# RWKV scan of a hybrid layer on one core: every product of a chunk as 64x64 tiles on the array's diagonal

## The chip, the cores and the metric

One core of one Trainium2 chip runs the whole layer in one launch. The time is device microseconds of that core. PE is the engine of the matrix products, DVE and ACT work element by element, POOL does the rest, SP issues transfers.

## The reference, cut to what matters

One layer normalises its input, projects it once, runs three kinds of heads side by side (gated DeltaNet, RWKV-7, Mamba-2) and projects their outputs back. All is float32. The change lies in the RWKV heads (8 of width 64) and, for a small part, in the DeltaNet heads (6 of width 128).

```
def rwkv7_recurrence(r, w, k, v, a, b):          # state S is 64x64 for each head
    def step(state, inp):
        sa = einsum("bhvk,bhk->bhv", state, a_t)
        state = state * w_t + sa[..., None] * b_t + v_t[..., None] * k_t
        return state, einsum("bhvk,bhk->bhv", state, r_t)
...
def gated_delta_rule(q, k, v, g, beta):          # chunks of 64; 1040 frames with the meta tokens
    a_mat = where(strict, einsum("bhnid,bhnjd->bhnij", kb, k) * dmask, 0.0)
    sol = triangular_solve(a_mat + eye(CHUNK), rhs, left_side=True, lower=True, unit_diagonal=True)
```

## The kernel before, in words

A planner (`schedule`) walks through twelve units (six of DeltaNet, a0 to a5; four of RWKV, b0 to b3, of two heads each; two of Mamba, c0 and c1) and lays their steps out in one order. The projection's products (tile `pj`, at one pass in float32r) are the filling: a unit runs until a `yield`, the planner notes how long its result will take on ACT or DVE, and puts projection products until then. The costs are counted by `Meter`; for a float32 product it counts the larger of the moving and the stationary columns over 600. A priority then decides which instruction goes ahead where several could. PE works in that order.

A unit of RWKV (`unit_b`) has two heads, which lie on the two halves of the 128 rows of its tiles: rows 0 to 63 and rows 64 to 127. It has 17 chunks of 64 frames.

- `bn`: norms of the keys, one small product for each chunk.
- `bgr`: the chunk's matrices of inner products. For each head one product of 64 rows by 128 columns, with 128 moving columns (bk against ar, where the two halves of 128 are a and r, or b and k). DVE masks them into `bgm`.
- `bbT`, `bvT`: transposes, which ACT copies out to `bbt` and `buv`.
- `solve32` inverts 32x32 blocks on DVE. The merges `bm1` and `bm2` (products of 32x32) put the inverse of 64x64 together, chunk by chunk and head after head.
- The scan runs over the chunks. Into PSUM tile `bsi` go the product of `ar` with the state (128x128, with the state of both heads as a block diagonal) and for each head a product of 64x64; ACT copies it to `b_x`; `bu` is for each head a product of 64x64; DVE scales it into `buv`; `bd` is one product of 128x128, of which only the two diagonal blocks are used; ACT and DVE make the next state `b_s` of it (one DVE instruction for each head); and a product of 128 rows by 64 columns for each head adds to the outputs, which ACT copies to `by`.

A float32 product is two records in the trace, each with its own load of the stationary matrix; a transpose or a float32r product is one. In DeltaNet (`unit_a`) the merges are `am1` to `am3` (32x32) and `am4`, `am5` (64x64). Each lane of units has two PSUM buffers (`ps`).

Of the kernel before, what the change touches and what calls it, by code (L numbers as in the profile page):

```python
# [26 lines left out]
EPS = 1e-6  # L27
# [13 lines left out]
PIPE = 0.5  # L41
# [60 lines left out]
class Trunk:  # L102
# [266 lines left out]
    def unit_a(self, h):  # L369
        nc, sm = self.nc, self.sm  # L370
        v, act, pe, pool, sync = self.engines
        ident = self.ident
# [16 lines left out]
        lo3 = lo[:, NM:].rearrange("p (c t) -> p c t", c=8)  # L389
# [24 lines left out]
        bd = sm.tile([128, 9], F32, tag="a_bd", name="a_bd", bufs=3)  # L414
# [80 lines left out]
        yield  # L495
        v1 = dvf[:, 512:768], dvf[:, 0:256]
        fs = [(slice(64 * i, 64 * i + 32), slice(64 * i + 32, 64 * i + 64)) for i in range(2)]
        for i, (f, s) in enumerate(fs):
            p = self.ps(f"am1{h}_{i}")
            for c in range(8):  # L500
                pe.matmul(p[s, 32 * c: 32 * c + 32], lo3[f, c, s], dd[f, c, 0:32], start=True, stop=True)
            act.copy(v1[i][s], p[s, 0:256])
            yield 0.6
        for i, (f, s) in enumerate(fs):
            p = self.ps(f"am2{h}_{i}")
            for c in range(8):
                pe.matmul(p[f, 32 * c: 32 * c + 32], v1[i][s, 32 * c: 32 * c + 32], lo3[s, c, s], start=True, stop=True)
            act.copy(lo3[f, :, s], p[f, 0:256].rearrange("p (c t) -> p c t", c=8))
            if i == 0:
                yield 0.6  # L510
                p = self.ps(f"am3{h}")
                for c in range(8):
                    pe.matmul(p[s, 32 * c: 32 * c + 32], lo3[s, c, s], v1[0][s, 32 * c: 32 * c + 32], start=True, stop=True)
                act.copy(dd[s, :, 0:32], p[s, 0:256].rearrange("p (c t) -> p c t", c=8))
                yield 0.3
        yield

        f, s = slice(0, 64), slice(64, 128)
# [122 lines left out]
    def unit_b(self, p):  # L641
# [43 lines left out]

        ar, bk = ([self.one([128, 9 - i, 128], f"b{x}{p}_{i}") for i in range(2)] for x in ("ar", "bk"))

        ib = sm.tile([64, 17, 2], F32, tag="b_ib", name="b_ib")
        for i, (s, e) in enumerate(split):
            act.activation(bk[i][:, :, 0:64], k[:, s:e], AF.Square, scale=self.kk[:, p: p + 1])  # L690
        yield
        ps = self.ps(f"bn{p}")
        for c in range(17):
            pe.matmul(ps[0:64, 2 * c: 2 * c + 2], at_c(bk, c)[:, 0:64], self.blk[:, 0:65:64], start=True, stop=True)
        v.tensor_scalar(ib, ps[0:64, 0:34].rearrange("p (c h) -> p c h", h=2), EPS, None, ADD)
# [13 lines left out]
        yield 11  # L709
        self.calm = False  # L710

        gms = [[self.one([128, 9 - i, 128], f"bgm{p}_{h}{i}") for i in range(2)] for h in range(2)]
        gm = lambda h, c: at_c(gms[h], c)
        banks = ((1, 5), (5, 9), (9, 13), (13, 17), (0, 1))
        hs = (slice(0, 64), slice(64, 128))
        for s, e in banks:
            for h in range(2):
                ps = self.ps(f"bgr{p}_{h}{s}")
                for c in range(s, e):
                    pe.matmul(ps[:, 128 * (c - s): 128 * (c - s) + 128], at_c(bk, c)[hs[h]], at_c(ar, c)[hs[h]], start=True, stop=True)  # L720
                v.tensor_tensor(gms[h][s // 9][:, s % 9: s % 9 + e - s, :], ps[:, : 128 * (e - s)].rearrange("p (c t) -> p c t", c=e - s),
                                bc(self.maskb, 1, e - s), MUL)
                yield PIPE
        for h in range(2):
            for i, (s, e) in enumerate(split):
                ab = gms[h][i][0:64, :, 0:64]
                nc.vector.tensor_tensor(ab, ab, bc(ib[:, s:e, h], 2, 64), MUL)
# [9 lines left out]
        blocks = [(34 * h + 17 * b + s, e - s, gms[h][i][32 * b: 32 * b + 32, :, 32 * b: 32 * b + 32])  # L737
                  for h in range(2) for b in range(2) for i, (s, e) in enumerate(split)]
        for o, n, t in blocks:
            nc.sync.dma_start(d1[o: o + n].rearrange("c i j -> i c j"), t)  # L740
# [17 lines left out]
        for c in range(0, 17, 4):  # L758
            cc = range(max(c - 3, 0), c + 1)
            ps = self.ps(f"bvT{p}_{c}")  # L760
            for j in range(0, len(cc), 2):
                pe.transpose(ps[: 64 * min(2, len(cc)), 64 * j: 64 * j + 128], v_[:, 64 * cc[j]: 64 * (cc[j] + min(2, len(cc)))], ident)
            for j, x in enumerate(cc):
                h = slice(64 * (j % 2), 64 * (j % 2) + 64)
                act.copy(at_c(uv, x)[64:128], ps[h, 64 * (j - j % 2): 64 * (j - j % 2) + 128])
            yield PIPE

        for w in range(2):
# [4 lines left out]
            yield PIPE  # L773
        yield

        dv = self.one([128, 34, 32], f"bdd{p}")
        f, s = slice(0, 32), slice(32, 64)
        for h in range(2):
            for i, (c0, c1) in enumerate(split):
                nc.vector.transpose(dv[f, 17 * h + c0: 17 * h + c1, :], gms[h][i][f, :, f])  # L780
        self.lag += 4
        yield
        for i0, n in ((0, 9), (9, 8), (17, 9), (26, 8)):
            p1 = self.ps(f"bm1{p}_{i0}")
            for i in range(i0, i0 + n):
                pe.matmul(p1[s, 32 * (i - i0): 32 * (i - i0) + 32], gm(i // 17, i % 17)[f, s], dv[f, i, :], start=True, stop=True)
            act.copy(dv[s, i0: i0 + n, :], p1[s, : 32 * n].rearrange("p (c t) -> p c t", c=n))
            yield
            p2 = self.ps(f"bm2{p}_{i0}")
            for i in range(i0, i0 + n):  # L790
                pe.matmul(p2[f, 32 * (i - i0): 32 * (i - i0) + 32], dv[s, i, :], gm(i // 17, i % 17)[s, s], start=True, stop=True)
            act.copy(gms[i0 // 17][n % 9 // 8][f, :, s], p2[f, : 32 * n].rearrange("p (c t) -> p c t", c=n))
            yield 0.1
        yield 12


        yt = self.one([128, 8, 128], f"by{p}")
        st = None
        for c in range(17):
            pq = self.ps(f"bsi{p}_{c}")  # L800
            if c:
                pe.matmul(pq[:, 0:128], at_c(ar, c), st, start=True, stop=False, skip_group_check=True)
            for h in range(2):
                pe.matmul(pq[0:64, hs[h]], gm(h, c)[64:128, 0:64], at_c(uv, c)[64:128, hs[h]],
                          start=(c == 0), stop=True, skip_group_check=True)
# [4 lines left out]
            for h in range(2):  # L810
                pe.matmul(pu[0:64, hs[h]], gm(h, c)[0:64, 0:64], x[0:64, hs[h]], start=True, stop=True)
            v.tensor_tensor(at_c(uv, c)[0:64].rearrange("p (h d) -> p h d", h=2), pu[0:64, 0:128].rearrange("p (h d) -> p h d", h=2),
                            bc(ib[:, c, :], 2, 64), MUL)
            yield
            if c < 16:
                pd = self.ps(f"bd{p}_{c}")
                pe.matmul(pd[:, 0:128], at_c(bt, c), at_c(uv, c), start=True, stop=True)
                sn = self.tmp("b_s")
                if c:
                    nc.scalar.activation(sn, st, AF.Copy, scale=wc[:, c + 1: c + 2])  # L820
                    for h in range(2):
                        v.scalar_tensor_tensor(sn[hs[h], hs[h]], pd[hs[h], hs[h]], wc[hs[h], c + 1: c + 2], sn[hs[h], hs[h]], MUL, ADD)
                else:
                    nc.gpsimd.memset(sn, 0.0)
                    for h in range(2):
                        v.tensor_scalar(sn[hs[h], hs[h]], pd[hs[h], hs[h]], wc[hs[h], c + 1: c + 2], None, MUL)
            if c:
                for h in range(2):
                    pe.matmul(pq[64:128, hs[h]], gm(h, c)[:, 64:128], at_c(uv, c)[:, hs[h]],
                              start=False, stop=True, skip_group_check=True)  # L830
                nc.scalar.copy(yt[hs[(c - 1) % 2], (c - 1) // 2, :], pq[64:128, 0:128])  # L831
                self.lag = max(0.2, self.lag - 0.21)
            if c < 16:
                st = sn
            if c == GATE:
                yield 8
                g = self.one([128, 17, 64], f"bg{p}")
                gated = self.later(36 + p, self.shifted(36 + p, 12 + p, g, gate=True), DUES[4])
                g = flat(g)
            else:  # L840
                yield
# [536 lines left out]
```

## Time and profile before

| what | before |
|---|---|
| median of 3 runs | 1480.29 us (1477.94 to 1482.15) |
| the profiled execution | 1481.04 us |
| its span, first to last instruction | 1479.3 us |
| PE busy | 1420.0 us, 96% |
| DVE, ACT, POOL busy | 65%, 48%, 12% |
| mean granted clock of PE | 0.965 |

The span is what the profile shows; 1.7 us lie around it. A product counts as busy until its result is out, and the next one starts before that, so that a busy PE may still hold pauses: start to start says more than busy time. The granted clock is 1 at 2.4 GHz and 0.5 at 1.2 GHz.

### The profile page before, as it was taken

The page shows a single profiled execution, that of the slowest core. Times are in us where ns is not written, and L with a number is a line of the kernel's source. Part 1 is how long each engine was busy: PE and PEld are TensorE (multiplying, and loading weights), DVE is VectorE, ACT ScalarE, POOL GpSimd, SP SyncE. Part 2 cuts the span into 40 slices and gives each one's busy share as a digit, 9 for nine tenths or more (in the row PEclk, how much of TensorE's full clock was granted, in tenths as well). Part 3 has the DMA queues.
Part 4 walks back from the last instruction along what each step waited for, and adds up shares of the span by engine and source line. Part 5 has one row for each costly group of instructions (what it writes and reads, how often), then busy time and mean ns, then how long its engine had stood idle before and what let it go on. Part 6 is the DMA issues. An engine that isn't in the chain of part 4 may idle for free.

```text
span 1479.3 us, 25499 instructions
## 1 busy us (share of the span) xinstructions
PE 1420.0 (96%) x9369; PEld 1228.4 (83%) x9369; DVE 961.0 (65%) x2682; ACT 704.1 (48%) x1924; POOL 172.8 (12%) x227
## 2 busy tenths in 40 slices
PE   4999999999999999899899999999999999889897
PEld 4999888888888888878778899889998978678686
DVE  7549486376658557879745788556588866642573
ACT  6465272245434462454655644544566354632530
POOL 2111000000000110111101111001222000200100
PEclk9999799799999999999979999999999999899999
DMA  7344323133222332434422243333544322643851
GB/s 228 87 116 86 82 62 73 30 61 90 58 45 58 87 80 66 114 62 93 92 76 55 51 101 76 61 72 88 142 90 94 74 39 50 203 142 98 255 195 54
DMA packets 120447, 136.25 MB, mean 92 GB/s; under 512 B 39867, under 2 KB 72379, under 8 KB 120323
## 3 DMA queue, kind: packets, MB, share of 16 engines
q1 hardware_dynamic: 102755, 102.64, 23.8%
q0 software_dynamic: 17568, 31.99, 12.9%
q8 instruction: 74, 1.21, 0.4%
q14 instruction: 50, 0.41, 0.1%
HBM read 116.99 MB, written 17.60 MB: 91 GB/s over the span
## 4 chain that ended last, share of the span: by engine, by line
PE 78%; DVE 8%; DMA 6%; ACT 5%; issue 2%; POOL 0%; SPq 0%; DVEq 0%; ACTq 0%; POOLq 0%
PE pj L97 41%; PE po L97 9%; PE bsi L97 5%; PE am L97 2%; PE bgr L97 2%; PE bu L97 2%; DMA omrw<-d_mix 1%; PE bm L97 1%; PE aops L97 1%; PE bd L97 1%; PE cdg L97 1%; PE ads L97 1%; DMA x<-in_x_dram 1%; DVE s_tmp L97 1%; PE agq L97 1%
## 5 line engine op out<-in xcount | busy, mean ns | idle before, releaser
L97 PE MATMUL pj<-hh,w 128*128 128x350 f32 (+7 forms) x2736 | 756.8, 349 | 1.8 <-DMA w<-in_wt_dram 1.6
L97 PEld LDWEIGHTS pj<-hh,w 128*128 128x128 f32 x2736 | 486.7, 192 | 24.5 <-DMA w<-in_wt_dram 2.0
L97 PE MATMUL pj<-hl,w 128*128 128x350 f32 (+7 forms) x1368 | 477.4, 349 | 0.0
L97 PEld LDWEIGHTS pj<-hl,w 128*128 128x128 f32 x1368 | 262.0, 191 | 11.8 <-issue 0.5
L153 POOL DMA_DIRECT2D w<-in_wt_dram x122 | 106.8, 876 | 853.9 <-ACT w L151 697.0
L151 ACT ACTIVATE w<-wr 128x512 fp32r<-128x512 f32 x122 | 76.8, 629 | 87.5 <-PE pj L97 86.4
L97 PE MATMUL po<-ow,omw 128*128 128x512 f32 x408 | 95.4, 395 | 4.5 <-ACT omw L1067 3.7
L97 PEld LDWEIGHTS po<-ow,omw 128*128 128x128 f32 x408 | 77.4, 191 | 22.5 <-ACT omw L1067 4.1
L97 PE MATMUL po<-ow,ome 128*128 128x512 f32 x360 | 88.9, 400 | 2.1 <-ACT ome L1067 1.9
L97 PEld LDWEIGHTS po<-ow,ome 128*128 128x128 f32 x360 | 67.2, 190 | 16.1 <-ACT ome L1067 2.5
L152 ACT CAST w<-wr 128x512 fp32r<-128x512 f32 x122 | 74.3, 609 | 0.1
L97 DVE TENSOR_TENSOR buv<-bu,b_ib 64x128 f32<-64x128 f32 x68 | 19.1, 282 | 69.5 <-PE bu L97 69.1
L97 PE MATMUL bsi<-buv,bgm 64*64 64x64 f32 (+1 forms) x528 | 62.5, 239 | 0.0
L97 DVE TENSOR_TENSOR alb<-alb,s_tmp 33x30 f32<-33x30 f32 (+9 forms) x180 | 57.0, 317 | 3.0 <-POOL alb L97 1.6
L97 DVE TENSOR_TENSOR s_tmp<-alb 33x30 f32<-33x30 f32 (+9 forms) x180 | 56.9, 316 | 1.2
L97 PEld LDWEIGHTS bsi<-buv,bgm 64*64 64x64 f32 (+1 forms) x528 | 42.7, 140 | 17.7 <-issue 2.7
L831 ACT COPY by<-bsi 64x128 f32<-64x128 f32 x64 | 16.8, 263 | 77.1 <-PE bsi L97 76.5
L97 DVE SCALAR_TENSOR_TENSOR b_s<-bd,b_wc,b_s 64x64 f32<-64x64 f32 x120 | 33.9, 283 | 29.8 <-PE bd L97 27.4
L1068 DVE TENSOR_TENSOR ome<-omre,ome 128x512 fp32r<-128x512 f32 (+2 forms) x40 | 21.7, 581 | 39.4 <-ACT ome L1067 39.4
L97 ACT COPY b_x<-bsi 64x128 f32<-64x128 f32 x68 | 17.6, 259 | 60.4 <-PE bsi L97 59.9
L184 DVE SCALAR_TENSOR_TENSOR cbc<-pj,pack,cbc 128x346 f32<-128x346 f32 (+4 forms) x72 | 40.0, 569 | 8.5 <-ACT cbc L181 7.7
L97 DVE TENSOR_TENSOR blb<-blb,s_tmp 68x30 f32<-68x30 f32 (+14 forms) x120 | 38.3, 320 | 1.5
(325 smaller groups left out, 2450.6 us busy)
## 6 DMA issues: line engine op xcount, KB each, us to landing
wr<-in_wt_dram SPq DMA_DIRECT2D x122, 256.0 KB, 3.4
w<-in_wt_dram POOLq DMA_DIRECT2D x122, 256.0 KB, 4.8
or<-in_w_out_dram SPq DMA_DIRECT2D x32, 256.0 KB, 3.3
omrw<-d_mix SPq DMA_DIRECT2D x32, 256.0 KB, 4.6
clt<-d_cs SPq DMA_DIRECT2D x24, 256.0 KB, 4.7
omre<-d_mix SPq DMA_DIRECT2D x24, 256.0 KB, 4.1
btw<-d_tw SPq DMA_DIRECT2D x8, 544.0 KB
x<-in_x_dram SPq DMA_DIRECT2D x8, 512.0 KB, 7.6
```

The source lines that it names most:

```text
L97: return op(out, *args, **kw)
L151: nc.scalar.activation(w[:, 1], raw, AF.Copy, scale=-1.0)
L152: nc.scalar.copy(w[:, 0], raw)
L153: nc.gpsimd.dma_start(w[:, 1], src, accum_op=ADD)
L184: nc.vector.scalar_tensor_tensor(acc[:, a + z: b], p[:, o + z - s: o + b - a - s], cw[:, 3 - s: 4 - s], acc[:, a + z: b], MUL, ADD)
L831: nc.scalar.copy(yt[hs[(c - 1) % 2], (c - 1) // 2, :], pq[64:128, 0:128])
L1068: nc.vector.tensor_tensor(t[:, 1], raw, t[:, 0].bitcast(F32), SUB)
```

## The change

All products of an RWKV chunk become products of 64x64, one for each head: head 0 reads rows 0 to 63 and writes partitions 0 to 63, head 1 reads rows 64 to 127 and writes partitions 64 to 127, and the two stand one after the other in the program. Both write the same PSUM bank, on their own partitions. The index of `gms` is now the half of the columns (a or r) and no longer the head; a tile holds both heads on its two halves. The state is kept as 128 rows by 64 columns. ACT copies the transposes out in pieces of 64 rows, and the outputs in two pieces. The merges of both heads stand in turn, and so do those of DeltaNet's two 64-row halves, which go to two PSUM buffers.

```diff
@@ unit_a, merges
+        pair = [self.ps(f"am1{h}_{i}") for i in range(2)]
+        for c in range(8):
+            for i, (f, s) in enumerate(fs):
+                pe.matmul(pair[i][s, 32 * c: 32 * c + 32], lo3[f, c, s], dd[f, c, 0:32], start=True, stop=True)
         for i, (f, s) in enumerate(fs):
-            p = self.ps(f"am1{h}_{i}")
-            for c in range(8):
-                pe.matmul(p[s, 32 * c: 32 * c + 32], lo3[f, c, s], dd[f, c, 0:32], start=True, stop=True)
-            act.copy(v1[i][s], p[s, 0:256])
-            yield 0.6
+            act.copy(v1[i][s], pair[i][s, 0:256])
+        yield 0.6
...
@@ unit_b, bgr
-            for h in range(2):
-                ps = self.ps(f"bgr{p}_{h}{s}")
-                for c in range(s, e):
-                    pe.matmul(ps[:, 128 * (c - s): 128 * (c - s) + 128], at_c(bk, c)[hs[h]], at_c(ar, c)[hs[h]], start=True, stop=True)
+            pair = [self.ps(f"bgr{p}_{x}{s}") for x in range(2)]
+            for c in range(s, e):
+                for x in range(2):
+                    for h in range(2):
+                        pe.matmul(pair[x][hs[h], 128 * (c - s): 128 * (c - s) + 128], at_c(bk, c)[hs[h], hs[x]], at_c(ar, c)[hs[h]],
+                                  start=True, stop=True)
...
@@ unit_b, transposes out
-            act.copy(bt[s // 9][:, s % 9: s % 9 + e - s, :], ps[:, : 128 * (e - s)].rearrange("p (c t) -> p c t", c=e - s))
+            for x in range(2):
+                for h in range(2):
+                    act.copy(bt[s // 9][hs[h], s % 9: s % 9 + e - s, hs[x]],
+                             ps[hs[x], : 128 * (e - s)].rearrange("p (c t) -> p c t", c=e - s)[:, :, hs[h]])
...
@@ unit_b, scan
+            def both(out, cols, lhs, part, rhs, start, stop):
+                for h in range(2):
+                    pe.matmul(out[hs[h], cols], lhs[hs[h], part], rhs[hs[h]], start=start, stop=stop, skip_group_check=True)
+
             pq = self.ps(f"bsi{p}_{c}")
+            both(pq, hs[0], gk, to_a, v1_, True, c == 0)
             if c:
-                pe.matmul(pq[:, 0:128], at_c(ar, c), st, start=True, stop=False, skip_group_check=True)
...
+                both(pq, hs[0], a_r, to_a, st, False, True)
+                both(pq, hs[1], gk, to_r, v1_, True, False)
+                both(pq, hs[1], a_r, to_r, st, False, False)
             x = self.tmp("b_x")
-            act.copy(x[0:64], pq[0:64, 0:128])
+            act.copy(x[:, 0:64], pq[:, 0:64])
...
+            both(pu, hs[0], gb, to_a, x[:, 0:64], True, True)
+            if c < 16:
+                pd = pu[:, 64:128]
+                both(pu, hs[1], b_k, hs[1], v1_, True, False)
+            v.tensor_scalar(u_, pu[:, 0:64], ib[:, c: c + 1], None, MUL)
...
-                pe.matmul(pd[:, 0:128], at_c(bt, c), at_c(uv, c), start=True, stop=True)
+                both(pu, hs[1], b_k, hs[0], u_, False, True)
...
-                    for h in range(2):
-                        v.scalar_tensor_tensor(sn[hs[h], hs[h]], pd[hs[h], hs[h]], wc[hs[h], c + 1: c + 2], sn[hs[h], hs[h]], MUL, ADD)
+                    v.scalar_tensor_tensor(sn[:, 0:64], pd, w_, sn[:, 64:128], MUL, ADD)
...
+                both(pq, hs[1], gb, to_r, u_, False, True)
                 for h in range(2):
-                    pe.matmul(pq[64:128, hs[h]], gm(h, c)[:, 64:128], at_c(uv, c)[:, hs[h]],
-                              start=False, stop=True, skip_group_check=True)
-                nc.scalar.copy(yt[hs[(c - 1) % 2], (c - 1) // 2, :], pq[64:128, 0:128])
+                    nc.scalar.copy(yt[hs[(c - 1) % 2], (c - 1) // 2, hs[h]], pq[hs[h], 64:128])
```

What stands on PE around chunk 10 of unit b0's scan before (`bsi0_10` is unit 0, chunk 10; a row names what is written, then moving and stationary operand, then the output's partitions and columns):

```order
L97 MATMUL bsi0_10_3061<-b_s_3048,bar0_1_1213 128x128
L97 MATMUL bsi0_10_3061<-buv0_1_2268,bgm0_01_1468 64x64
L97 MATMUL bsi0_10_3061<-buv0_1_2268,bgm0_11_1470 64x64
L97 MATMUL pj33_1_3186<-hh_79,w33_1_2950 128x386 x2
L97 MATMUL pj33_1_3186<-hl_80,w33_1_2950 128x386
L97 MATMUL bu0_10_3078<-b_x_3065,bgm0_01_1468 64x64
L97 MATMUL bu0_10_3078<-b_x_3065,bgm0_11_1470 64x64
L97 MATMUL pj33_1_3186<-hh_79,w33_1_2950 128x386
L97 MATMUL pj33_2_3256<-hh_79,w33_0_2944 128x322
L97 MATMUL pj33_2_3256<-hl_80,w33_0_2944 128x322
L97 MATMUL pj33_2_3256<-hh_79,w33_0_2944 128x322
L97 MATMUL bd0_10_3087<-buv0_1_2268,bbt0_1_1603 128x128
```

The chunk goes on with the two products into the outputs, so that it has 8 products in three shapes, with three or four of the projection between its three places.

And now, around chunk 9 and the start of chunk 10:

```order
L97 MATMUL bu0_9_3280<-b_x_3268,bgm0_01_1484 64x64 x2
L97 MATMUL bu0_9_3280<-buv0_1_2450,bbt0_1_1630 64x64 x2
L97 MATMUL pj33_1_3214<-hh_79,w33_1_3126 128x386
L97 MATMUL pj33_1_3214<-hl_80,w33_1_3126 128x386
L97 MATMUL pj33_1_3214<-hh_79,w33_1_3126 128x386
L97 MATMUL bu0_9_3280<-buv0_1_2450,bbt0_1_1630 64x64 x2
L97 MATMUL bsi0_9_3259<-buv0_1_2450,bgm0_01_1484 64x64 x2
```

Each `x2` of 64x64 is now a pair, head 0 and head 1. A chunk's 8 products became 16, in eight pairs of one shape; there are three projection products between two places here.

What stands on PE for the second bank of `bgr` of unit b0 before (`bgr0_05` is head 0, `bgr0_15` head 1, of four chunks each):

```order
L97 MATMUL pj25_2_1805<-hh_79,w25_0_1412 128x322 x2
L97 MATMUL pj25_2_1805<-hl_80,w25_0_1412 128x322
L97 MATMUL bgr0_05_1491<-bar0_0_1212,bbk0_0_1214 128x128 x4
L97 MATMUL bgr0_15_1501<-bar0_0_1212,bbk0_0_1214 128x128 x4
L97 MATMUL pj25_2_1805<-hh_79,w25_0_1412 128x322 x2
L97 MATMUL pj25_2_1805<-hl_80,w25_0_1412 128x322
```

The four products of head 0 stand ahead of the four of head 1, and each head has a PSUM buffer of its own.

And now (`bgr0_05` is the a half, `bgr0_15` the r half, of both heads):

```order
L97 MATMUL bgr0_05_1514<-bar0_0_1212,bbk0_0_1214 64x128 x7
L97 MATMUL bgr0_15_1515<-bar0_0_1212,bbk0_0_1214 64x128 x6
L97 MATMUL bgr0_05_1514<-bar0_0_1212,bbk0_0_1214 64x128
L97 MATMUL bgr0_15_1515<-bar0_0_1212,bbk0_0_1214 64x128 x2
L97 MATMUL pj25_2_1862<-hh_79,w25_0_1429 128x322
L97 MATMUL pj25_2_1862<-hl_80,w25_0_1429 128x322
```

Eight products of 64 by 128 became sixteen of 64 by 64, with as many moving columns each, and the heads stand in turn.

## Rows read from the trace of the kernel before

**Rows 1.** The page: its span, and PE, DVE and ACT's busy time.

```profile
span 1479.3 us, 25499 instructions
PE 1420.0 (96%) x9369; PEld 1228.4 (83%) x9369; DVE 961.0 (65%) x2682; ACT 704.1 (48%) x1924; POOL 172.8 (12%) x227
...
PE 78%; DVE 8%; DMA 6%; ACT 5%; issue 2%; POOL 0%; SPq 0%; DVEq 0%; ACTq 0%; POOLq 0%
```

**Rows 2.** Span and mean granted clock.

```profile
core 0: 1479.3 us, clock 0.965
```

**Rows 3.** Groups by shape on PE: count, busy us, mean ns, idle time before.

```profile
L97 PE MATMUL bgr<-bar,bbk 64*128 64x128 f32 x272 | 38.3, 318 | 0.0
L97 PE MATMUL bsi<-buv,bgm 64*64 64x64 f32 x272 | 32.6, 238 | 0.0
L97 PE MATMUL bu<-b_x,bgm 64*64 64x64 f32 x272 | 31.9, 238 | 0.2 <-ACT b_x L97 0.2
L97 PE MATMUL bsi<-buv,bgm 128*64 128x64 f32 x256 | 29.9, 240 | 0.0
L97 PE MATMUL bd<-buv,bbt 128*128 128x128 f32 x128 | 27.1, 295 | 0.0
L97 PE MATMUL bsi<-b_s,bar 128*128 128x128 f32 x128 | 26.5, 290 | 0.0
L97 PE MATMUL bm<-bdd,bgm 32*32 32x32 f32 x272 | 13.0, 193 | 0.8 <-DVE bdd L780 0.8
L97 PE MATMUL bn<-pack,bbk 128*64 128x2 f32 x136 | 9.8, 203 | 0.0
```

**Rows 4.** Timeline of PE in a scan: start, length, records in a row.

```profile
575.63 0.38 PE L97 MATMUL bsi<-b_s,bar 128*128 128x128 f32 x2
575.94 0.44 PE L97 MATMUL bsi<-buv,bgm 64*64 64x64 f32 x4
576.31 0.44 PE L97 MATMUL pj<-hh,w 128*128 128x386 f32 x1
576.59 0.33 PE L97 MATMUL pj<-hl,w 128*128 128x386 f32 x1
576.76 0.52 PE L97 MATMUL pj<-hh,w 128*128 128x386 f32 x2
577.21 0.44 PE L97 MATMUL bu<-b_x,bgm 64*64 64x64 f32 x4
```

**Rows 5.** Timeline of PE: two pairs of rows that differ in their count alone.

```profile
747.95 0.61 PE L97 MATMUL agq<-aq,ak 128*128 128x128 f32 x4
748.51 0.39 PE L97 MATMUL agq<-aq,ak 128*128 128x128 f32 x2
...
1185.31 1.14 PE L97 MATMUL am<-add,alo 64*64 64x64 f32 x16
927.04 1.02 PE L97 MATMUL am<-alo,add 64*64 64x64 f32 x14
```

**Rows 6.** Timeline of PE: inner products, heads one after the other, and mixed.

```profile
150.39 1.71 PE L97 MATMUL bgr<-bar,bbk 64*128 64x128 f32 x16
245.39 1.16 PE L97 MATMUL bgr<-bar,bbk 64*128 64x128 f32 x14
```

**Rows 7.** Timeline of PE: merges alone, and in turn (20 single rows from 751.75).

```profile
238.60 0.75 PE L97 MATMUL bm<-bgm,bdd 32*32 32x32 f32 x18
...
751.75 0.21 PE L97 MATMUL bm<-bgm,bdd 32*32 32x32 f32 x1
751.76 0.21 PE L97 MATMUL bm<-bdd,bgm 32*32 32x32 f32 x1
...
752.07 0.19 PE L97 MATMUL bm<-bdd,bgm 32*32 32x32 f32 x1
```

**Rows 8.** Stretches: length, projection's PE busy (count), PEld, ACT, POOL, granted clock, DMA.

```profile
252.60:279.60 27.00, 4.78 (x13) 2.96 (x13) 1.14 (x2) 0.88 (x1) 0.50 0.16 30
280.00:340.00 60.00, 42.27 (x197) 30.39 (x195) 5.79 (x10) 4.30 (x5) 1.00 0.29 59
420.00:440.00 20.00, 5.55 (x19) 3.14 (x20) 0.00 (x0) 0.00 (x0) 1.00 0.12 22
757.80:774.50 16.70, 7.13 (x13) 3.97 (x14) 1.24 (x2) 0.88 (x1) 0.50 0.10 16
```

**Rows 9.** Groups by shape on DVE and ACT.

```profile
L97 DVE SCALAR_TENSOR_TENSOR b_s<-bd,b_wc,b_s 64x64 f32<-64x64 f32 x120 | 33.9, 283 | 29.8 <-PE bd L97 27.4 <-ACT avt L97 0.4
L97 ACT COPY b_x<-bsi 64x128 f32<-64x128 f32 x68 | 17.6, 259 | 60.4 <-PE bsi L97 59.9
L831 ACT COPY by<-bsi 64x128 f32<-64x128 f32 x64 | 16.8, 263 | 77.1 <-PE bsi L97 76.5
L97 ACT COPY bbt<-bbT 128x512 f32<-128x512 f32 x16 | 9.1, 588 | 14.2 <-PE bbT L97 14.1
```

More of the change, by code (lines that the diff above doesn't have):

```diff
@@ L497, in unit_a @@
         fs = [(slice(64 * i, 64 * i + 32), slice(64 * i + 32, 64 * i + 64)) for i in range(2)]
+        pair = [self.ps(f"am1{h}_{i}") for i in range(2)]
+        for c in range(8):
+            for i, (f, s) in enumerate(fs):
+                pe.matmul(pair[i][s, 32 * c: 32 * c + 32], lo3[f, c, s], dd[f, c, 0:32], start=True, stop=True)
         for i, (f, s) in enumerate(fs):
[L499 to L515 removed]
+            act.copy(v1[i][s], pair[i][s, 0:256])
+        yield 0.6
+        pair = [self.ps(f"am2{h}_{i}") for i in range(2)]
+        for c in range(8):
+            for i, (f, s) in enumerate(fs):
+                pe.matmul(pair[i][f, 32 * c: 32 * c + 32], v1[i][s, 32 * c: 32 * c + 32], lo3[s, c, s], start=True, stop=True)
+        f, s = fs[0]
+        for c in range(8):
+            pe.matmul(pair[0][s, 32 * c: 32 * c + 32], lo3[s, c, s], v1[0][s, 32 * c: 32 * c + 32], start=True, stop=True)
+        act.copy(dd[s, :, 0:32], pair[0][s, 0:256].rearrange("p (c t) -> p c t", c=8))
+        for i, (f, s) in enumerate(fs):
+            act.copy(lo3[f, :, s], pair[i][f, 0:256].rearrange("p (c t) -> p c t", c=8))
         yield
@@ L757, in unit_b @@
         uv = [self.one([128, 9 - i, 128], f"buv{p}_{i}") for i in range(2)]
[L758 to L765, printed above, removed]
+        for s, e in ((0, 1), (1, 9), (9, 17)):
+            ps = self.ps(f"bvT{p}_{s}")
+            n, m = (e - s + 1) // 2, min(e - s, 2)
+            for j in range(n):
+                pe.transpose(ps[: 64 * m, 128 * j: 128 * j + 128], v_[:, 64 * (s + 2 * j): 64 * (s + 2 * j + m)], ident)
+            for j in range(m):
+                for h in range(2):
+                    x = s % 9 + j
+                    act.copy(uv[s // 9][hs[h], x: x + 2 * n - 1: 2, 64:],
+                             ps[hs[j], : 128 * n].rearrange("p (c t) -> p c t", c=n)[:, :, hs[h]])
             yield PIPE
@@ L774, in unit_b @@
         yield
-        dv = self.one([128, 34, 32], f"bdd{p}")
-        f, s = slice(0, 32), slice(32, 64)
-        for h in range(2):
+        dv = self.one([128, 17, 32], f"bdd{p}")
+        fs = [(slice(64 * h, 64 * h + 32), slice(64 * h + 32, 64 * h + 64)) for h in range(2)]
+        f0, s0 = slice(0, 32), slice(32, 64)
+        for f, _ in fs:
             for i, (c0, c1) in enumerate(split):
-                nc.vector.transpose(dv[f, 17 * h + c0: 17 * h + c1, :], gms[h][i][f, :, f])
+                nc.vector.transpose(dv[f, c0: c1, :], gms[0][i][f, :, f0])
         self.lag += 4
         yield
[L783 to L787, printed above, removed]
-            yield
[L789 to L792, printed above, removed]
+        for i, (c0, c1) in enumerate(split):
+            n = c1 - c0
+            flat_c = lambda ps: ps[:, : 32 * n].rearrange("p (c t) -> p c t", c=n)
+            p1 = self.ps(f"bm1{p}_{i}")
+            for c in range(n):
+                for f, s in fs:
+                    pe.matmul(p1[s, 32 * c: 32 * c + 32], gms[0][i][f, c, s0], dv[f, c0 + c, :], start=True, stop=True)
+            for f, s in fs:
+                act.copy(dv[s, c0: c1, :], flat_c(p1)[s])
+            yield
+            p2 = self.ps(f"bm2{p}_{i}")
+            for c in range(n):
+                for f, s in fs:
+                    pe.matmul(p2[f, 32 * c: 32 * c + 32], dv[s, c0 + c, :], gms[0][i][s, c, s0], start=True, stop=True)
+            for f, s in fs:
+                act.copy(gms[0][i][f, :, s0], flat_c(p2)[f])
             yield 0.1
@@ L797, in unit_b @@
         yt = self.one([128, 8, 128], f"by{p}")
-        st = None
+        st, to_a, to_r = None, hs[0], hs[1]
         for c in range(17):
+            gb, gk, a_r, b_k, uvc = (at_c(t, c) for t in (gms[0], gms[1], ar, bt, uv))
+            u_, v1_ = uvc[:, 0:64], uvc[:, 64:]
+            def both(out, cols, lhs, part, rhs, start, stop):
+                for h in range(2):
+                    pe.matmul(out[hs[h], cols], lhs[hs[h], part], rhs[hs[h]], start=start, stop=stop, skip_group_check=True)
```

41 lines of the change are left out of this document (16 added, 25 removed).

## Prediction, on record before the changed kernel ran

> **What bounds the kernel now.** I read the page first: PE is busy for 1420.0 of 1479.3 us, and the chain that ended last lies on it for 78% [rows 1]. DVE (65%) and ACT (48%) have room. So the time is the sum of what PE's products take, and I ask of each edit what it does to that sum. Busy time overstates a single group, since a product counts until its result is out. What counts is start to start, and for that I read the timeline.
>
> Four things are to be seen in it. First, the pace of one tile of the array. Two rows that differ by two records give it: (0.61 - 0.39) / 2 = 0.11 us for a record with 128 columns, and (1.14 - 1.02) / 2 = 0.06 us for one of 64x64 [rows 5].
>
> Second, two tiles on different rows run at the same time. Eighteen merges of one tile take 0.75 us; less the 0.19 us that the last one stays busy, 17 steps of 0.033 us. Where two tiles stand in turn, 20 records start between 751.75 and 752.07, 0.017 us apart [rows 7]. The inner products show it too: less 0.30 us for the last, 16 records with the heads one after the other come 1.41 / 15 = 0.094 us apart, 14 mixed ones 0.86 / 13 = 0.066 [rows 6], against 0.11 alone.
>
> Third, a change of tile size costs. Two records of 128 take 0.31 us to the next start instead of 0.22; four of 64 then 0.37 instead of 0.24; the projection's first record 0.28, where the next one takes 0.17 [rows 4]. Together 0.09 + 0.13 + 0.11 = 0.33 us for a visit to smaller tiles and back.
>
> Fourth, the clock. The mean of 0.965 [rows 2] means that 1479.3 x 0.035 = 52 us of full speed are missing. The two longest half-speed stretches are 27 us around 266 us and 16.7 us around 766 us [rows 8]; there PE did little projection work (4.8 of 27 us, 7.1 of 16.7) and many small products, while the scan at 280 to 340 us, with 42 of 60 us, ran at full clock. But 420 to 440 us kept full clock with 5.6 of 20 us, so projection's share does not decide alone.
>
> **The change, part by part.**
>
> *Scan.* Before: 272 + 272 + 256 = 800 records with 64 columns at 0.06 us and 128 + 128 = 256 with 128 at 0.11 [rows 3, 5]: 48.0 + 28.2 = 76.2 us. Now the order has 1040 products, 2080 records, and 1011 of the products stand next to one of the other head. If pairs run together, 1040 pairs x 0.06 = 62.4 us. **-14 us.** That a 64x64 pair runs at the pace of one tile is carried over from the merges and the inner products [rows 6, 7]; these went to two PSUM banks, the new pairs write one. No row of before has that case. The bounds: fully together, -14; one after the other, 124.8 us, +49.
>
> *Inner products.* Before, 272 records [rows 3] at some 0.08 us (between the 0.094 and the 0.066 of [rows 6]) are 22 us. Now they are 544 records of half the width with the same 128 moving columns; 272 pairs at 0.11 are 30 us. **+8 us** (bounds: +0 if before had no overlap, +15 if all of it). The row tiles of before filled all 128 columns and overlapped already; the diagonal uses half of the array.
>
> *Merges of RWKV.* 127 of 272 products stood next to one of another row tile, now 257. At 0.033 alone and 0.0165 in turn: before 290 x 0.033 + 254 x 0.0165 = 13.8 us, now 30 x 0.033 + 514 x 0.0165 = 9.5. **-4 us.** *Merges of DeltaNet:* though written in turn, only 48 of 240 products stand so in the order against 21: 54 records x 0.0165. **-1 us.** *Norms:* 136 records become 136 pairs [rows 3], 0.
>
> *Changes of tile size.* Counted over PE's whole order: 750 before, 744 now; three visits x 0.33. **-1 us.** I had expected more here: the scan has one shape less, but projection products still part its three places in each chunk.
>
> *DVE, ACT, POOL.* DVE makes the state in one instruction in place of two: 60 x 0.283 = 17 us less [rows 9]. ACT gets more: 64 output copies (0.263) become 128 smaller ones, up to +17 us, and 16 copies of bbt (0.588) become 64 of half the rows and half the columns; with the 0.26 of the 64x128 rows as floor and half of 0.588 as a second guide they take 17 to 19 us in place of 9 [rows 9], +9. Neither is the bound: ACT would stand near 49%. On the path from `bsi` to `bu` lie the product's 0.24 us, the copy of 0.26 [rows 3, 9] and some 0.1 for the hand-over, 0.6 us. The order puts between them the pairs for the outputs (8 records, 0.24 us) and at least two projection products with their change of size (0.33 + 2 x 0.17): 0.9 us. So the copies' cover holds; without it a chunk would cost up to 0.6 us, 68 chunks 41 us. The two buffers of `bgr` are now taken as a pair, but in the order the next pair stands some ten projection products later, 1.7 us, behind two masks of some 0.7 us.
>
> Sum: -14 + 8 - 4 - 1 - 1 = **-12 us**. The profiled execution took 1481.04 us (span 1479.3, 1.7 around it), 0.75 above the median of the runs; 1481 - 12 = **1469 us**.
>
> **What speaks against it.** The new pairs write one bank from two row tiles at a time. The Trainium skill's page "TensorEngine Tiling (Array Packing)", section "Gotcha 1: PSUM Pressure", says that different row tiles write to different PSUM banks and cannot use the same bank simultaneously. By that rule the pairs would run one after the other, and the sum would be that of the rival "one after the other" below instead of -12. No row of before has two row tiles in one bank, so the trace neither bears it out nor refutes it for halves that share no partition.
>
> **Rivals.**
>
> *Heads one after the other.* Place: each of the 1040 + 272 + 136 = 1448 pairs. Price: 62 us (scan) + 272 x 0.11 = 30 (inner products) + 8 (norms) + 8 (merges, whose pairs now share a bank as well): 1469 + 108 = 1577 us. It decides early: 12 / 1448 = 8 ns more for each pair and the gain is gone. For it speaks that no row shows a shared bank; against it that each head has its own partitions, and that a full 128x128 product writes all of them in one bank anyway. Chance 0.07; it is the one whose price the page's rule would set.
>
> *More time at half clock.* The scans now have less projection work between places (three products where three or four stood) and no full-array product. If one whole scan fell to 1.2 GHz as the stretch at 252.6 did [rows 8], but for 44 us, 22 us are lost: 1469 + 22 = 1491. It decides from 2 x 12 = 24 us more of half clock on. For it: the scan's own products now fill half of the array at most. Against it: the scans at 280 us and at 420 us kept the clock. Chance 0.18.
>
> *Less time at half clock.* The cluster before the fall at 252 us mixed inner products, merges and scan with a change of size every few records. In the new order those merges take fewer places. If both long stretches go, (27 + 16.7) / 2 = 22 us come back: 1469 - 22 = 1447. Chance 0.18.
>
> *Nothing in the sum.* Pairs of the scan overlap only in part (short runs of four or eight records), the inner products cost the upper bound: 1477 to 1485. Chance 0.15.
>
> **How the numbers follow.** My forecast has 0.42, with its own range 1458 to 1476.5. Faster by over 0.3% (4.4 us, about what runs of this kernel can tell from no change): forecast and less half clock, 0.60. Same 0.15. Slower: more half clock and one after the other, 0.25. The range leaves out the heads one after the other and what lies beyond one clock case: 1447 with 5 us for the merges' and inner products' bounds below it, 1442, to 1492.
>
> **What the changed profile would show.** Scan: the 64x64 rows of `bsi` and `bu` with 16 records in about 0.7 us instead of 1.14; if they take 1.2, the heads run one after the other. Inner products: 32 records in about 2 us. Two DVE groups of `b_s` become one of half the count. The granted clock, 0.965 before, tells the clock rivals apart: 0.95 or less is the slower one, 0.98 the faster. What would make me wrong is above all the shared bank, then the clock.

## The result, and the profile after

The changed kernel takes 1446.55 us (median of 4 runs, 1442.08 to 1453.09), before 1480.65 beside it: 0.977 times, 95% interval 0.9743 to 0.9797. It is 34 us faster, where 12 were forecast. The profiled execution took 1442.35 us. In all that follows, four runs that took over 1.5% longer than the fastest of their kernel are left out of the medians: three of e1's six, its profiled one among them, and one of e3's four.

The page after, and the granted clock, to be held against [rows 1, 2]:

```profile
span 1440.4 us, 28351 instructions
PE 1389.7 (96%) x10801; PEld 1188.8 (83%) x10801; DVE 935.4 (65%) x2610; ACT 719.9 (50%) x2020; POOL 172.4 (12%) x223
...
core 0: 1440.4 us, clock 0.985
```

Three numbers split the 38.9 us between the two spans. Missing at half clock: 1479.3 x 0.035 = 51.8 before, 1440.4 x 0.015 = 21.6 now, **-30**. Time in which PE was not busy: 1479.3 - 1420.0 = 59.3 before, 1440.4 - 1389.7 = 50.7 now, **-9**. That leaves next to nothing for the sum of the products, on which the forecast rested.

PE's groups by shape after, for [rows 3]:

```profile
L97 PE MATMUL bsi<-buv,bgm 64*64 64x64 f32 x784 | 63.0, 230 | 0.7 <-DVE b_s L97 0.2
L97 PE MATMUL bgr<-bar,bbk 64*64 64x128 f32 x544 | 45.4, 277 | 0.0
L97 PE MATMUL bu<-buv,bbt 64*64 64x64 f32 x512 | 42.4, 234 | 0.0
L97 PE MATMUL bsi<-b_s,bar 64*64 64x64 f32 x512 | 38.6, 226 | 0.0
L97 PE MATMUL bu<-b_x,bgm 64*64 64x64 f32 x272 | 23.6, 244 | 1.2 <-ACT b_x L97 1.0
```

Their busy times overlap, so I added up start to start on PE, less pauses, less half of what lies in half-speed stretches. In us, before and after: scan 115.7 and 97.2; inner products 30.9 and 37.0; merges of RWKV 18.0 and 11.7, of DeltaNet 31.9 and 29.7; projection 776.5 and 789.1; output products 178.0 and 182.8; the rest 221.4 and 221.8. Together 1372.1 and 1369.2: **-3**. (By the same count half speed cost 47.4 and 20.1, pauses 40.0 and 31.6.) The smaller products take 21 us less, projection and output products 17 more.

Where projection's increase comes from is seen in the timeline of PE in a chunk, beside [rows 4]. First after, then before:

```profile
285.41 0.28 PE L97 MATMUL bsi<-buv,bgm 64*64 64x64 f32 x4
285.53 0.28 PE L97 MATMUL bsi<-b_s,bar 64*64 64x64 f32 x4
285.74 0.42 PE L97 MATMUL pj<-hh,w 128*128 128x336 f32 x1
286.00 0.32 PE L97 MATMUL pj<-hl,w 128*128 128x336 f32 x1
286.15 0.32 PE L97 MATMUL pj<-hh,w 128*128 128x336 f32 x1
286.40 0.33 PE L97 MATMUL bu<-b_x,bgm 64*64 64x64 f32 x4
286.57 0.28 PE L97 MATMUL bu<-buv,bbt 64*64 64x64 f32 x4
286.78 0.42 PE L97 MATMUL pj<-hh,w 128*128 128x336 f32 x1
```

```profile
293.60 0.32 PE L97 MATMUL pj<-hl,w 128*128 128x350 f32 x1
293.76 0.33 PE L97 MATMUL pj<-hh,w 128*128 128x350 f32 x1
294.01 0.44 PE L97 MATMUL bu<-b_x,bgm 64*64 64x64 f32 x4
```

Four records, two pairs, take 0.12 us (285.41 to 285.53), half of the 0.06 each that a single tile needs [rows 5]. The last projection product ahead of a pair takes 0.25 us to the next start (286.15 to 286.40), and the last one ahead of single 64x64 products took 0.25 us before (293.76 to 294.01). Over all such places at full speed the median is 0.251 us, before (50 places) and now (192). So a change of tile size costs projection what it did, but more of the changes stand next to it. Before, two of a chunk's three places in the scan began with a 128x128 product, which follows projection without a change, and the scan's own product bore the change to 64x64 (0.205 us instead of 0.109, 59 places at full speed). Of PE's 750 changes before and 744 now, 162 and 264 come right behind a projection product, 332 and 229 behind one of the scan; and 254 and 287 come right ahead of a projection product. These 135 more, at some 0.1 us each, are about projection's 12.6 us. Most of what projection gained in changes the scan lost, so the two have to be read together: -18.5 + 12.6 = **-6 us**.

The stretches at which I had looked, projection's part in them (columns as in [rows 8]):

```profile
239.00:245.80 6.80, 5.07 (x17) 4.61 (x18) 0.00 (x0) 0.00 (x0) 0.50 0.01 2
252.00:280.00 28.00, 15.09 (x70) 11.13 (x70) 1.24 (x2) 0.86 (x1) 1.00 0.21 39
723.70:740.80 17.10, 7.07 (x11) 2.67 (x11) 1.14 (x2) 0.86 (x1) 0.50 0.17 32
```

The clock still falls behind the merges of b0, but it rises after 6.8 us instead of 27, in which projection was busy for 5.07; the 28 us from 252 now hold 15.1 us of projection at full clock, where 27 us held 4.8. The stretch behind the merges of b3 is as long as before. A third one, 17.1 us from 167 us before, is gone: the prediction had read 252 and 758 us as the two longest, but this one was as long as the second.

DVE and ACT, for [rows 9]:

```profile
L97 DVE SCALAR_TENSOR_TENSOR b_s<-bu,b_wc,b_s 128x64 f32<-128x64 f32 x60 | 16.9, 282 | 31.0 <-PE bu L97 25.3 <-PE bsi L97 2.7 <-ACT a_vn L97 1.8
L852 ACT COPY by<-bsi 64x64 f32<-64x64 f32 x128 | 26.5, 207 | 48.9 <-PE bsi L97 47.6
L97 ACT COPY bbt<-bbT 64x256 f32<-64x256 f32 x64 | 23.5, 367 | 4.4 <-PE bbT L97 3.6
L97 ACT COPY b_x<-bsi 128x64 f32<-128x64 f32 x68 | 14.4, 212 | 47.5 <-PE bsi L97 47.1
```

### The profile page after: what moved, and what is told of

Its sections match the earlier page's. It is cut to its first block, busy times and chain, and to the rows that moved or that the text cites. A ratio compares the mean times of both kernels' runs of the same rounds, so it can differ in the third digit from the quotient of the medians.

```text
span 1440.4 us, 28351 instructions
## 1 busy us (share of the span) xinstructions
PE 1389.7 (96%) x10801; PEld 1188.8 (83%) x10801; DVE 935.4 (65%) x2610; ACT 719.9 (50%) x2020; POOL 172.4 (12%) x223
## 4 chain that ended last, share of the span: by engine, by line
PE 78%; issue 6%; ACT 6%; DMA 4%; DVE 4%; POOL 0%; SPq 0%; DVEq 0%; ACTq 0%; POOLq 0%
PE pj L97 45%; PE po L97 5%; PE bsi L97 4%; PE bu L97 3%; PE bgr L97 3%; PE am L97 2%; PE aops L97 1%; PE cdg L97 1%; ACT bbt L97 1%; DMA or<-in_w_out_dram 1%; PE ads L97 1%; PE av L97 1%; DMA omrw<-d_mix 1%; PE aks L97 1%; PE agk L97 1%
## 5 line engine op out<-in xcount | busy, mean ns | idle before, releaser
L97 DVE TENSOR_SCALAR buv<-bu,b_ib 128x64 f32<-128x64 f32 x68 | 19.2, 282 | 71.6 <-PE bu L97 71.5
L97 PE MATMUL bsi<-buv,bgm 64*64 64x64 f32 x784 | 63.0, 230 | 0.7 <-DVE b_s L97 0.2
L97 PEld LDWEIGHTS bsi<-buv,bgm 64*64 64x64 f32 x784 | 43.5, 136 | 16.5 <-issue 4.6
L184 DVE SCALAR_TENSOR_TENSOR cbc<-pj,pack,cbc 128x346 f32<-128x346 f32 (+4 forms) x72 | 41.1, 571 | 20.5 <-ACT cbc L181 19.7
L852 ACT COPY by<-bsi 64x64 f32<-64x64 f32 x128 | 26.5, 207 | 48.9 <-PE bsi L97 47.6
L97 PE MATMUL bgr<-bar,bbk 64*64 64x128 f32 x544 | 45.4, 277 | 0.0
L97 PE MATMUL bu<-buv,bbt 64*64 64x64 f32 x512 | 42.4, 234 | 0.0
L184 DVE SCALAR_TENSOR_TENSOR cx<-pj,pack,cx 128x346 f32<-128x346 f32 (+2 forms) x54 | 31.1, 576 | 16.9 <-ACT cx L181 15.9
```

The costliest lines, as they stand in the source:

```text
L97: return op(out, *args, **kw)
L184: nc.vector.scalar_tensor_tensor(acc[:, a + z: b], p[:, o + z - s: o + b - a - s], cw[:, 3 - s: 4 - s], acc[:, a + z: b], MUL, ADD)
L852: nc.scalar.copy(yt[hs[(c - 1) % 2], (c - 1) // 2, hs[h]], pq[hs[h], 64:128])
```

## Experiments

Theory A: most of the gain is clock, fewer and shorter half-speed stretches. Rival B: that is luck of the order, which any small shift would move. Rival C: the gain is the overlap of the pairs. "Full-speed span" is span times granted clock, the median over the runs. The two columns on the right are read from one trace of each kernel.

| kernel | median us | ratio to before, 95% | clock | full-speed span | longest half-speed stretch, 225 to 320 us | same, 1220 to 1320 us |
|---|---|---|---|---|---|---|
| before (61 runs; profile) | 1482 | | 0.965 | 1428 | 27.3 | 10.2 |
| after | 1446.6 | 0.977 (0.974 to 0.980) | 0.982 | 1418 | 6.8 | 3.4 |
| e1 RWKV alone | 1457.0 | 0.983 (0.979 to 0.988) | 0.977 | 1419 | 6.8 | 10.2 |
| e2 DeltaNet alone | 1519.7 | 1.029 (1.025 to 1.033) | 0.958 | 1452 | none | none |
| e3 scan, heads apart | 1464.7 | 0.989 (0.986 to 0.992) | 0.981 | 1435 | 6.8 | 3.4 |
| e4 inner, heads apart | 1474.6 | 0.996 (0.994 to 0.998) | 0.979 | 1441 | 6.8 | 3.4 |
| e5 before, 0.25 | 1524.2 | 1.028 (1.025 to 1.031) | 0.945 | 1441 | 20.5 | 17.1 |
| e6 before, 0.35 | 1470.7 | 0.993 (0.990 to 0.995) | 0.970 | 1424 | 27.3 | 10.2 |
| e7 after, 0.25 | 1445.9 | 0.976 (0.972 to 0.980) | 0.982 | 1416 | 3.4 | 3.4 |
| e8 after, 0.35 | 1455.8 | 0.983 (0.979 to 0.987) | 0.978 | 1420 | 6.8 | 6.8 |
| e9 before, spread | 1530.0 | 1.031 (1.026 to 1.037) | 0.954 | 1458 | 10.2 | 10.2 |
| e10 merges apart | 1443.1 | 0.974 (0.970 to 0.977) | 0.985 | 1421 | 6.8 | 3.4 |
| e11 count halved | 1441.1 | 0.973 (0.967 to 0.979) | 0.986 | 1418 | 6.8 | 3.4 |
| e12 DeltaNet spread | 1490.6 | 1.004 (1.001 to 1.007) | 0.966 | 1436 | 3.4 | 3.4 |
| e13 before, filled | 1495.6 | 1.012 (1.009 to 1.015) | 0.959 | 1432 | 34.1 | 17.1 |
| e14 before, pairs | 1497.2 | 1.010 (1.003 to 1.017) | 0.957 | 1432 | 27.3 | 17.1 |
| e15 after, halves | 1448.1 | 0.980 (0.977 to 0.982) | 0.982 | 1419 | none | 3.4 |
| e16 before, quads | 1484.9 | 1.000 (0.998 to 1.002) | 0.962 | 1427 | 23.9 | 17.1 |
| e17 after again | 1446.7 | 0.975 (0.972 to 0.978) | 0.982 | 1419 | 6.8 | 3.4 |
| e18 count halved again | 1442.6 | 0.972 (0.968 to 0.976) | 0.986 | 1419 | 6.8 | 3.4 |

**One part alone.** In e1 `unit_a`'s merges are those of before, in e2 they alone are changed.

e1: 

> The changed kernel with DeltaNet's merges in their old order. Clock theory (most of the 34 us are half-speed stretches that RWKV's new order does without; clock 0.985 after, 0.965 before): the RWKV part carries it, 1443 to 1455 us, clock 0.98 to 0.99. Rival, luck of the planner's order: any small change moves the half-speed stretches, so the clock lies anywhere from 0.96 to 0.985 and the time up to 1475. Rival, array (the time comes from overlapped pairs alone): within 3 us of the changed kernel whatever the clock.

e2: 

> The kernel before with only DeltaNet's merges in turn. Clock theory: half speed comes from RWKV's products, so the clock stays at 0.965 +- 0.004 and the time at 1473 to 1483 us (the merges in turn give 1 to 3 us). Luck of the order: clock anywhere from 0.96 to 0.985, time 1450 to 1485.

RWKV's part gives the whole full-speed gain (1419). How much of the clock it gives is less sure: e1's six runs lie between 1448 and 1475 us, at clocks from 0.965 to 0.981, wider apart than those of the changed kernel. What DeltaNet's merges add to it is not shown (the two intervals overlap); by themselves they cost some 40 us. So the parts don't add up. In e2 the cost is a wait, as PE's waits show:

```profile
PE pj L97 <- DVE s_tmp L97: 24.8, 1, 24.8
...
PE pj L97 <- DVE cx L187: 9.7, 1, 9.7
```

Projection stood still for 24.8 us until DVE, busy with the 32x32 inverses (`s_tmp`), was through. The new order brings other pieces of work together on DVE; no step of the prediction looked there.

**Heads apart.** e3 collects the products of a place and issues them head after head; e4 makes the head the outer loop:

```diff
 e3, scan
             def both(out, cols, lhs, part, rhs, start, stop):
                 for h in range(2):
-                    pe.matmul(out[hs[h], cols], lhs[hs[h], part], rhs[hs[h]], start=start, stop=stop, skip_group_check=True)
+                    todo[h].append((out[hs[h], cols], lhs[hs[h], part], rhs[hs[h]], start, stop))
...
+                for one in todo:
+                    for o_, l_, r_, s_, e_ in one:
+                        pe.matmul(o_, l_, r_, start=s_, stop=e_, skip_group_check=True)
...
 e4, inner products
-            for c in range(s, e):
-                for x in range(2):
-                    for h in range(2):
+            for h in range(2):
+                for c in range(s, e):
+                    for x in range(2):
```

e3: 

> The changed kernel, in each place of the scan first all products of head 0 and then all of head 1. Array theory: the pairs no longer overlap except at the seam; a record of 64x64 costs 0.06 us again, 2080 x 0.06 = 125 us against the 62 of the pairs, less what one seam for each place keeps (about a third): +35 to +60 us over the changed kernel at the same clock, 1480 to 1505. Rival (the scan's waits set its pace, not its products): within 8 us of the changed kernel.

e4: 

> The changed kernel, in each bank of the inner products first head 0 and then head 1. Array theory: 544 records of 0.11 us instead of 272 pairs: +30 us at the same clock, about 1475. Clock theory adds: the stretch of small products grows by that much and may fall to half speed, clock 0.975 or less, up to 1490. Rival (the inner products lie beside other waits): within 8 us of the changed kernel.

The full-speed spans rise by 17 and 23 us, so pairs that share a bank do overlap. The scan's rise is far under the 35 expected: a place is short, and at the seam of two heads and at the change of tile size the time is spent either way (328 of the scan's 1040 products still follow one of the other head, after 781). The clock stays at 0.981 and 0.979. So the overlap keeps the 64x64 form from costing some 40 us more, but the clock doesn't hang on it, and against the old form the products gain 3 us in all: C explains neither the clock nor most of the 34 us.

**The planner shifted a little.** The allowance `LATE` is 0.25 or 0.35 in place of 0.3, before (e5, e6) and after (e7, e8).

e5: 

> The kernel before with the planner's allowance for lateness at 0.25 us instead of 0.3, which shifts where its filling goes. Span times granted clock (what the span would be at full speed) is 1427 to 1431 us for before. Theory that the half-speed stretches belong to the old form of RWKV's products: clock 0.960 to 0.970, 1473 to 1488 us. Rival, luck of the order: the clock leaves that band on either side, up to 0.985, and the time follows it (1455 at 0.982).

e6: 

> The same with 0.35 us. Old form: clock 0.960 to 0.970, 1473 to 1488 us. Luck of the order: a clock outside of that band, the time following it by 1.5 us for each 0.001.

e7: 

> The changed kernel with the allowance at 0.25 us. Full-speed span 1417 to 1421 us as after. New form keeps the clock: 0.976 to 0.987, 1438 to 1456 us. Luck of the order: a clock down to 0.965, 1470 us.

e8: 

> The changed kernel with 0.35 us. New form keeps the clock: 0.976 to 0.987, 1438 to 1456 us. Luck of the order: a clock down to 0.965, 1470 us.

B is right in part: this edit, which changes no product, moved before to 0.945 and 0.970 and its time by +43 and -10 us. But by the medians neither order of before reached 0.977, and neither order of after fell below it. Another edit brought it there: e12 below has the new products of both parts and a clock of 0.966.

**Pauses and counts.** e9 makes the pause behind each bank of inner products longer in before, e12 those between DeltaNet's merges in after; e10 issues RWKV's merges head after head; e11 and e18 halve the planner's count of the small products, and e17 is the changed kernel beside e18.

```diff
 e9, inner products of before
-                yield PIPE
+                yield 1.5
 e12, DeltaNet's merges (the plain yields there likewise)
-        yield 0.6
+        yield 2.5
 e11, e18
-            max(n, args[0].shape[-1]) / 600
+            max(n, args[0].shape[-1]) / (1200 if out.shape[0] == 64 else 600)
```

e9: 

> The kernel before with a longer pause after each bank of the inner products (1.5 of the planner's lag in place of 0.5), so that more projection products stand between the banks; no product is added or taken away. Theory that a long half-speed stretch comes where the planner leaves too few full-array products between small ones: the 27 us at 252 us shrink to 7 us or less as in the changed kernel, clock 0.972 to 0.980, 1460 to 1472 us, the full-speed span still 1427 to 1432. Rival (the shape of RWKV's products alone keeps the clock down): the stretch stays, clock 0.965, 1478 to 1486 us.

e10: 

> The changed kernel with RWKV's merges head after head. Array theory: 544 records at 0.033 instead of 0.017 us each, +4 to +9 us at the same clock, 1450 to 1456. Clock theory adds: more time with a single 32x32 tile at work, clock 0.970 to 0.980, up to 1470. Rival (merges hidden behind waits): no change, 1443 to 1450.

e11: 

> The changed kernel with the planner counting products that write 64 partitions at half, which is nearer to what pairs take, so that it puts more projection between RWKV's places. Theory that the planner's overcount is what changed the order: the order moves back towards that of before and the clock falls to 0.965 to 0.975, 1455 to 1475 us. Rival (the count doesn't matter): 1440 to 1456 us, clock 0.977 to 0.985.

e12: 

> The changed kernel with longer pauses between the steps of DeltaNet's merges (2.5 of the lag in place of 0.6 and 1), so that more projection stands between them. Theory as in the run of before with spread banks: the 17 us at half speed at 724 us shrink, clock 0.985 to 0.990, 1432 to 1442 us. Rival (projection is only moved, and is missing elsewhere): clock 0.975 to 0.985, 1442 to 1455 us.

e17: 

> The changed kernel itself, beside the next one on the same chip: 1442 to 1455 us, clock 0.977 to 0.985, the stretch near 724 us again 10 to 25 us long.

e18: 

> The changed kernel with the planner counting products that write 64 partitions at half, for a comparison with it on the same chip. If the shorter half-speed stretches of its first profile (none near 724 us) belong to its order: 1436 to 1445 us, clock 0.984 to 0.990, 5 to 8 us under the changed kernel. If they were that one execution's: within 3 us of the changed kernel.

In e9 the long stretch did shrink, to 10.2 us at 307, but a longer one stood at 747 us (37.5 us), and projection waited for DVE elsewhere, as in e2, and in e12 it did so in one wait. The first row is e9's, the second e12's:

```profile
PE pj L97 <- DVE av L187: 16.1, 1, 16.1
```

```profile
PE pj L97 <- DVE av L187: 20.0, 1, 20.0
```

In both the full-speed span rose (1458 and 1436) and the clock fell. In e10 RWKV's merges head after head take 16.3 us start to start instead of 11.7, but the kernel's time doesn't show it. The halved count did not bring the old clock back; beside each other its kernel took 1442.6 (1434.7 to 1453.6), the changed one 1446.7 (1446.2 to 1448.3), with overlapping intervals: whether it is better stays open.

**What makes the stretch at 252 us long.** e13 adds products of full size to unit b0, whose results nobody reads (they share the banks of the merges and of the scan, and its output is no longer the layer's; only its time is used here). e14 takes the banks of before's inner products as a pair, e16 also splits them into 64x64 products on all four quarters of the array; e15 undoes the pairing in after. In the cuts `cols` stands for the chunk's 128 columns, and the comments are not in the code.

```diff
 e13, before
+        def fill(t, o, n):
+            for _ in range(n if p == 0 else 0):
+                nc.tensor.matmul(t[:, o:512], self.hh[:, 0, 0:128], self.hh[:, 0, 0: 512 - o], start=True, stop=True, skip_group_check=True)
... behind each group of merges (p1, p2), and behind the first products of a chunk
+            fill(p1, 288, 4)
...
+            if c < 4:
+                fill(pq, 128, 4)
 e14, before
-                yield PIPE                       # behind each head's bank
+            yield PIPE                           # behind both, heads in turn
 e16, on top of e14
-                    pe.matmul(pair[h][:, cols], at_c(bk, c)[hs[h]], ...)
+                    pe.matmul(pair[h][hs[x ^ h], cols], at_c(bk, c)[hs[h], hs[x ^ h]], ...)     # x = 0, 1
 e15, after
-            yield PIPE                           # behind both halves
+                yield PIPE                       # behind each half
```

e13: 

> The kernel before with 48 extra products of full array size in one pass, whose results nobody reads: 4 behind each of unit b0's eight groups of merges (224 moving columns) and 4 in each of the first four chunks of its scan (384 columns). They add about 32 x 0.1 + 16 x 0.17 = 6 us of work and some changes of tile size, up to 5 us more. Theory that half speed follows a lack of full-array products: the 27 us at 252 us shrink to 10 or less, 8 to 12 us come back there, clock 0.970 or more; the time lies within 5 us of before although work was added, and the full-speed span rises by 6 to 11 us. Rival (full-array products have no part in it): stretch unchanged, clock 0.965 or less, 1488 to 1493 us.

e14: 

> The kernel before, where the inner products keep their 64x128 form but the banks of both heads are taken as a pair, with the heads in turn and one pause for both, as the changed kernel has it. Theory that this arrangement, and not the 64x64 form, shortened the stretch at 252 us: the stretch falls to 10 us or less, clock 0.970 or more, inner products some 5 to 10 us shorter as well (two full row tiles overlap), 1455 to 1470 us. Rival (the form of the scan's products): stretch of 20 us or more, clock 0.960 to 0.967, 1470 to 1482 us. Rival, luck of the order: stalls of over 60 us in sum and a slower kernel.

e15: 

> The changed kernel, where the inner products' two column halves are issued one after the other with a pause of their own behind each, as the heads were before. Theory that the arrangement in pairs shortened the stretch at 252 us: it returns with 15 us or more, clock 0.965 to 0.975, 1458 to 1472 us. Rival (the form, whatever the pauses): stretch of 7 us, clock 0.977 to 0.987, 1440 to 1456 us.

e16: 

> The kernel before with the pairs of e14 and with the inner products as 64x64 products, two for each head, heads in turn on different rows and columns of the array; everything else (scan, merges, DeltaNet) as before. Theory that the 64x128 form of the inner products draws the long stretch at half speed: no stretch over 10 us between 235 and 330 us, clock above e14's 0.957 by 0.006 or more, 1470 to 1486 us, full-speed span 3 to 8 us above e14's 1432 for the longer products. Rival (the scan's form, or the merges'): the stretch of 20 us or more remains, clock 0.950 to 0.962, 1490 to 1510 us.

Projection in those stretches, in e13, e14, e16 and, for the same place at full clock, in e15 (columns as above):

```profile
247.20:281.30 34.10, 0.69 (x1) 0.29 (x1) 0.00 (x0) 0.00 (x0) 0.50 0.05 9
```

```profile
250.50:277.80 27.30, 7.88 (x20) 5.12 (x20) 1.14 (x2) 0.88 (x1) 0.50 0.04 6
```

```profile
245.20:269.10 23.90, 6.91 (x17) 4.44 (x17) 1.05 (x2) 0.01 (x1) 0.50 0.07 12
```

```profile
235.00:270.00 35.00, 15.90 (x66) 10.01 (x65) 2.27 (x4) 1.74 (x2) 1.00 0.28 58
```

The added products in e13 pushed projection out of the stretch (0.69 us) and the stretch grew; so work of full size put in by hand did not help, and the theory of e9 and e13 is not borne out in that form. Pairing the banks (e14), splitting the inner products (e16) and undoing the pairing (e15) change little at this place. By the table the stretch is 20 us or more in six of eight kernels with RWKV's old form and 6.8 or less in all twelve with the new.

But the old form alone doesn't make it: in e2 and e9, where RWKV's products are those of before, it is gone. What tells the kernels apart is the order around b0's merges. The inner products of b1 that lie between b0's first merge and its last, in before, after, e2 and e9 (columns: length, PE busy (count), PEld, DVE, granted clock, DMA):

```profile
237.20:259.90 22.70, 8.17 (x44) 5.46 (x44) 3.36 (x5) 0.84 0.29 77
```

```profile
230.30:239.40 9.10, 3.12 (x14) 1.31 (x14) 0.00 (x0) 0.98 0.40 88
```

```profile
232.10:240.60 8.50, 0.00 (x0) 0.00 (x0) 0.00 (x0) 1.00 0.58 125
```

```profile
227.50:236.20 8.70, 0.00 (x0) 0.00 (x0) 0.00 (x0) 1.00 0.60 122
```

In the six kernels with 20 us or more, b0's merges are drawn out over 14 to 38 us, with 42 to 68 records of b1's inner products among them; in the other fourteen they take 8.5 to 11.3 us, with at most 16. So the stretch goes with this order, and RWKV's new form is one way to it. That is read off the twenty traces afterwards: no run moves these inner products alone. The stretch at 1250 us goes with DeltaNet's merges: 10.2 to 17.1 in the eight kernels with the old ones (e1 among them), at most 6.8 in the twelve with the new.

## Why the prediction was right and wrong

- **The clock: this step failed.** The sum took it as unchanged, with no term of its own, and gave "less time at half clock" 0.18. By the runs' medians the full-speed span fell from 1428 to 1418, and the other 24 us of the 34 are clock, 0.965 to 0.982. That rival's 1447 is where the time came out, partly by luck: it named the right cluster (252 us, shorter by 20 us) and a wrong second one, for the stretch at 758 us stayed. Instead the stretch at 167 us went (17.1 us before, none now) and that at 1250 us shrank.
- **The sum, -12, came out at -3,** though its parts had their sign: scan -18 (forecast -14), inner products +6 (+8), merges of RWKV -6 (-4), of DeltaNet -2 (-1). **The scan** was sized too large: with the changes of tile size that went from it to projection it gave -6, where -14 for its products and -1 for the changes stood. The count of the changes (750 and 744) and their price held, so these 9 us are not a dearer change: some 3 of them are changes that the two took over from other groups (33 more on either side of their products, at 0.1), and where the rest lies is open. The output products' +5 is not explained either (0.227 us a record before, 0.232 to 0.233 now, of the same shape).
- **Luck in the full-speed span:** its fall by 10 us looks like the forecast's 12, but the products gave 3 of it and shorter pauses the rest. By its products alone, 1481 - 3 = 1478, the change belongs to the rival "nothing in the sum" (1477 to 1485). Of that rival's two reasons, inner products at the upper bound did not come true (+6); whether the scan's pairs overlap only in part is not settled, with the rest of those 9 us.
- **Pauses** stood nowhere in the sum; 8 to 9 us less.
- **The shared bank** held: two pairs take 0.12 us, and heads apart cost 17 us. The rival "heads one after the other" (1577) is out. The rule of the Trainium skill's page "TensorEngine Tiling (Array Packing)", section "Gotcha 1: PSUM Pressure", that different row tiles cannot use one bank simultaneously, is not borne out by these 0.12 us for two tiles on the diagonal that write different partitions of it.
- **ACT:** outputs 26.5 us where up to 34 were allowed; `bbt` grew more than forecast (23.5 us in the row above alone, 17 to 19 forecast for all). Neither showed, as the cover argument said: PE waited 1.0 us for `b_x` in all 68 chunks. `b_s` went from 120 to 60 instructions.
- **Not settled:** why the clock follows that order, and which of RWKV's edits (scan, inner products, half as many groups of merges) makes the planner lay it out so. The scan's form alone was not tried, since the layout of the state, the transposes and the inner products goes with it.

## What to carry to other kernels

Where an engine is busy for 96% and its mean clock is 0.965, the 52 us of clock weigh more than an edit worth 12: give the clock a term with a size and a chance of its own, stretch by stretch, before forecasting "unchanged". An edit that moves a planner's order should be timed in two or three orders (a planner constant shifted a little, before and after), since here one and the same set of products moved by 43 us. And when two groups border on each other, add them up together: a change of tile size that leaves one group can turn up in the other, and then neither group's time says what the edit was worth.

## What the runs showed of the hardware

- A projection product of 350 columns takes 0.16 us to the next start, and 0.25 us when 64x64 products come next, whether on one tile (before) or as a pair on two (after).
- Two 64x64 products, on two tiles on the array's diagonal, that write different partitions of one PSUM bank run together: 0.06 us for a pair, as for one tile alone.
- Inner products on all four quarters, two banks (e16) took 30.3 us start to start at full speed, as long as the 64x128 form (29.4 in e14); on the diagonal alone they take 37.0, and 52.5 with the heads apart.
- One kernel on one chip spread from 1434.7 to 1453.6 us (e18) with a clock from 0.990 to 0.977 at a full-speed span that stayed within 1418 to 1422.
